# Seven small stores on SyncE's queue for one large store on ScalarE's, in a hybrid transformer block on one core

## The chip, the cores and the metric

The kernel runs on one core of one Trainium2 chip. The metric is the device time of one execution in microseconds. A profiled execution also gives the span, which is the time from its first instruction to its last.

## The reference

One layer with f32 inputs, a sequence of 512 tokens and a model width of 2048. The last three lines are the feed-forward part in which most of the time is spent; there `D_FF` is 5632.

```python
u = rmsnorm(x, attn_norm_w)
z, xbc, dt_raw, q, kc, vc, ks, vs, kw, vw, gate_raw = split(u @ w_in)
y_ssd = ssd_mixer(z, xbc, dt_raw, ...)
y_att = nsa_mixer(q, kc, vc, ks, vs, kw, vw, gate_raw, ...)
h = x + concatenate([y_ssd, y_att]) @ w_out
v = rmsnorm(h, ffn_norm_w)
h = h + (silu(v @ w_gate) * (v @ w_up)) @ w_down
return rmsnorm(h, final_norm_w)
```

## The kernel before

**Arithmetic.** A float32 product is made from three TensorE products of rounded values: each operand is split into a high part (written by ScalarE, line 124) and a low part (the rest, by VectorE, line 127). The three products are the lines 1223 to 1225, or 1219 where they are issued as one stream. The large matrix products are cut into quads of blocks that are multiplied with seven block products instead of eight (Strassen in Winograd's form). So each operand needs seven "forms", sums and differences of its blocks. For a weight, a form is one block as loaded, or a block onto which a second DMA adds another (line 1158 loads on SyncE's queue, line 1160 adds on GpSimd's), or a sum made by GpSimd or VectorE (line 136).

**Stages.** In the trace the input projection and the two mixers take the first 804 us. The output projection (`w_out`) runs from there to 857 us, the gate and up projections to 1735 us, the down projection to about 2180 us, and then the last norm and the output.

**Gate and up.** The 5632 columns are done in `NP` = 22 pairs of 256, about 40 us each. A pair is 14 steps of 16 matmuls. A small scheduler, `Sched`, counts two matmuls as a tick, so that a step has 8 ticks. Jobs such as `g_forms` are generators: `yield n` puts their next part n ticks later. So the ticks fix the order of the instructions on every engine at build time, and on the chip each engine takes its own in that order.

**Forms of a pair.** After a pair, `g_forms(u)` makes the seven forms of its activations, high and low part, in the staging area `ST`, which is part of the tile `A` (slots 44 to 71 of `A`). One DMA of 1792 KB on ScalarE's queue (line 1492) stores all seven to `g_d[u]` in DRAM. The down projection reads them back into a ring with seven slots (`GRING`; slots lie in the tiles `V`, `T` and `u`): pairs 0 to 4 from ScalarE's queue in loads of four and three forms (line 1580), later pairs form by form from SyncE's (line 1598).

**Weights.** `place` gives each coming weight block a buffer in zones of the tiles `Z`, `E` and `A` as soon as one is free, and the load is issued there. `P2["A2"]`, slots 70 to 75 of `A`, is one more zone for the down projection; `down_before` opens it at the visit `v` = 1. The down projection is a written-out list of 35 visits, each with weight blocks 384 to 768 columns wide.

**The output projection's evictions.** `ev_oa(c)`, for c from 0 to 15, adds the residual to a block of `h` (VectorE), stores it to `h_d` (line 1273, 256 KB, on GpSimd's queue), makes the next stage's forms from it, and loads the block c + 4 of the residual into the same buffer (line 1267), which has to wait until the store has read it. Four buffers go round.

**Queues and semaphores.** A DMA queue issues in program order, so what waits at its head holds back all behind it. The DMAs that SyncE and ScalarE issue carry eight completion semaphores in turn, counted over both queues in program order; each is made to wait until the DMA eight before it has landed.

Of the kernel before, what the change touches and what calls it, by code (L numbers as in the profile page):

```python
# [9 lines left out]
F32R = mybir.dt.float32r  # L10
# [7 lines left out]
NP = NFF // 2  # L18
# [7 lines left out]
GRING = 7  # L26
# [88 lines left out]
def body(ctx, tc, xT, w_in, w_out, w_gate, w_up, w_down, w1k, w1v, cols, rows, kst, out):  # L115
    nc = tc.nc
    act, dve, pool, pe = nc.scalar, nc.vector, nc.gpsimd, nc.tensor
    sch = Sched()

    def f(ap):  # L120
        return ap.bitcast(F32)

    def a_hi(dst, src, scale=1.0):
        act.activation(dst, src, AF.Copy, scale=scale)  # L124

    def lo(eng, dst, src, hi):
        eng.tensor_tensor(dst, src, f(hi), ALU.subtract)  # L127

    def neg_lo(dst, src, hi):
        dve.scalar_tensor_tensor(dst, src, -1.0, f(hi), op0=ALU.mult, op1=ALU.subtract)  # L130
# [4 lines left out]
    def add(eng, o, a, b):  # L135
        eng.tensor_tensor(o, a, b, ALU.add)  # L136
# [17 lines left out]
    def ps_v():  # L154
        return ps("v", 1)
# [9 lines left out]
    h_d = dram.tile([NJ, 128, 4, 256], F32, name="h_d")  # L165
    g_d = dram.tile([NP, 7, 128, 512], F32, name="g_d")
# [3 lines left out]
    def open_pool(name, stack=None, **kw):  # L170
        es = ExitStack()
        pools[name] = (es, es.enter_context(tc.tile_pool(name=name, bufs=1, reuse_waits="tile", **kw)))
        return pools[name][1]

    def close_pool(name):
        pools.pop(name)[0].close()
# [95 lines left out]
    def col(c, n=1):  # L272
        return colc[:, c:c + n]
# [311 lines left out]
    P2 = {}  # L585
# [677 lines left out]
    def load_h1(c):  # L1263
        if c < KD:
            P2["h1", c] = (P2["HH"][:, 0:2].rearrange("p a t -> p (a t)"), P2["HH"][:, 2:4].rearrange("p a t -> p (a t)"),
                           P2["SR"].rearrange("p a t -> p (a t)"), rrow)[c % 4]
            (nc.scalar if c < 4 else nc.sync).dma_start(P2["h1", c], h1_d[c])

    def ev_oa(c):
        def ev(p):  # L1270
            h = P2.pop(("h1", c))
            add(dve, h, p, h)
            nc.gpsimd.dma_start(h_d[c // 2][:, 2 * (c % 2):2 * (c % 2) + 2, :].rearrange("p a t -> p (a t)"), h)
            t = P2["t", c % 2] = P2["TT"][:, 2 * (c % 2):2 * (c % 2) + 2].rearrange("p a t -> p (a t)")
            a_hi(t, h, scale=col(C_FN + c))
            if c == 0:
                act.activation(acc2, h, AF.Square)
            else:
                q = ps_v()
                act.activation(q, h, AF.Square)  # L1280
                add(dve, acc2, q, acc2)
            k = c // 2
            if c % 2 == 0:
                a_hi(P2["V0"][:, k, 0, :], t[:, 0:256])
                lo(dve, P2["V0"][:, k, 1, :], t[:, 0:256], P2["V0"][:, k, 0, :])
            else:
                e = P2["t", 0]
                vh, t2 = P2["VV"][:, :, k, 0, :], t.rearrange("p (a t) -> p a t", a=2)
                a_hi(vh, t2)
                lo(dve, P2["VV"][:, :, k, 1, :], t2, vh)  # L1290
                t1, t2 = P2["T1"][k // 4][:, k % 4, :], P2["T2"][:, k, :]
                pool.tensor_tensor(t1, e[:, 256:512], e[:, 0:256], ALU.subtract)
                pool.tensor_tensor(P2["T34"][:, 0, k, :], e[:, 256:512], t[:, 256:512], ALU.subtract)
                pool.tensor_tensor(t2, t1, t[:, 256:512], ALU.subtract)
                pool.tensor_tensor(P2["T34"][:, 1, k, :], t[:, 0:256], t2, ALU.add)
            load_h1(c + 4)
            sch.flags.add(("oa", c))
            if c == 7:
                sch.add(half_t())
        return ev  # L1300
# [14 lines left out]
    def half_t():  # L1315
        yield 12
        t_piece(0, 0)
        yield 16
        t_piece(1, 0)
# [151 lines left out]
    def g_forms(u):  # L1471

        ct = P2["CT"].rearrange("p (s c a) t -> p s c (a t)", s=2, c=2)
        g = ct[:, 1]
        tg = ct[:, 0].rearrange("p a t -> p (a t)").rearrange("p (a t) -> p a t", a=4)
        sg = P2["ST"][:, 0:14, :].bitcast(F32R).rearrange("p (v s) t -> p v s t", s=2)
        yield 10
        a_hi(sg[:, 0, 0, :], g[:, 0, lo_h])
        a_hi(sg[:, 1:3, 0, :], g[:, 1, :].rearrange("p (a t) -> p a t", a=2), scale=-1.0)
        gq = g.rearrange("p c (a t) -> p (c a) t", a=2)  # L1480
        dve.tensor_tensor(tg[:, 1, :], gq[:, 1, :], gq[:, 0, :], ALU.subtract)
        add(dve, tg[:, 2, :], gq[:, 1, :], gq[:, 3, :])
        add(dve, tg[:, 0, :], tg[:, 1, :], gq[:, 3, :])
        dve.tensor_tensor(tg[:, 3, :], tg[:, 0, :], gq[:, 2, :], ALU.subtract)
        yield 4
        lo(dve, sg[:, 0, 1, :], g[:, 0, lo_h], sg[:, 0, 0, :])
        neg_lo(sg[:, 1:3, 1, :], g[:, 1, :].rearrange("p (a t) -> p a t", a=2), sg[:, 1:3, 0, :])
        a_hi(sg[:, 3:7, 0, :], tg)
        yield 4
        lo(dve, sg[:, 3:7, 1, :], tg, sg[:, 3:7, 0, :])  # L1490
        yield 16
        nc.scalar.dma_start(g_d[u].rearrange("v p n -> p v n"), f(sg).rearrange("p v s t -> p v (s t)"))
        sch.flags.add(("g", u))

    PIECES = {1: (1, 1), 4: (2, 0), 5: (2, 1), 7: (3, 0), 9: (3, 1)}
# [75 lines left out]
    def feed(i):  # L1571

        for half, r in ((0, slice(0, 4)), (1, slice(4, 7))):
            while nxt["ring", half] < 5:
                n = nxt["ring", half]
                at = done.get((n - GRING, 0), i) + 1 if half == 0 else done.get((4 - GRING, 0), i) + 3 + n // 2
                if at > i:
                    break
                G[n] = P2["slot"][n]
                nc.scalar.dma_start(f(G[n][:, r]).rearrange("p v s t -> p v (s t)"),  # L1580
                                    g_d[n, r].rearrange("v p n -> p v n"))
                nxt["ring", half] += 1
        if not ring:
            for n in range(5, NP):
                for o in range(7):
                    ring.append((first_use[n, o], n, o, later[n] if n < GRING else freed[n - GRING, o] + 3))
            ring.sort()
        here = [x for x in ring if x[3] <= i]
        tight = any(x[0] - 8 - i < k for k, x in enumerate(here, 1))
        for x in here[:2 if tight else 1]:  # L1590
            ring.remove(x)
            u, n, o, _ = x
            assert u > i + 4
            if n == NP - 1 and not o:
                sch.run_until(("g", n))
            G[n] = P2["slot"][n % GRING]
            a = G_POS[V_OF[SEQ_D[o]]]
            nc.sync.dma_start(f(G[n][:, a]).rearrange("p s t -> p (s t)"), g_d[n, a])
        if not ring:
            ring.append((len(steps) + 99, 0, 0, len(steps) + 99))  # L1600
# [3 lines left out]
    def add_h(v):  # L1604
        j = H_AT.get(v)
        if j is not None:
            assert all(x[0] != j for x in visits[v:v + 2]) and all(any(x[0] == j for x in y) for y in (visits[:v], visits[v + 2:]))
            nc.gpsimd.dma_start(P2["H"][j][:, 1:5, :], h_d[j], accum_op=ALU.add)

    def g_rhs(p, lo_):  # L1610
        a = G_POS[V_OF[p]]
        return lambda k: (G[lo_ + k][:, a, 0, :], G[lo_ + k][:, a, 1, :])
# [155 lines left out]
    def down_before(v, n):  # L1768
        def before():
            if n == 1:  # L1770
                assert v < NJ - 2 or not any(fz.busy[NZ2:])
                add_h(v)
                if v:
                    P2["A2"] = P2["A"][:, 70:76, :]
            elif n == 0 and v == 27:
                x = GRING * 2 + 1
                assert max(i for i, y in enumerate(visits) if y[1] <= x < y[2]) < v
                close_pool("t0")
                P2["X"] = open_pool("t0", side="right").tile([128, 32, 128], F32, name="X")
            elif (v, n) == (0, 0):  # L1780
                close_pool("E")
                P2["E2"] = P2["E"] = open_pool("E").tile([128, NE, 128], F32, name="E2")
        return before
# [13 lines left out]
    for v, (j, a, b) in enumerate(visits):  # L1797
# [14 lines left out]
        for n, p in enumerate(SEQ_D):  # L1812
            blk, sums = q["form"][p]
            if n == 0 and v in (2, 3):
                later[5 + (v == 3)] = len(items)
            s = Step(blk, g_rhs(p, a), bk(p), after=af(p),
                     before=down_before(v, n) if n < 2 else None, sums=sums)
# [54 lines left out]
    with tc.manual_schedule(engines={mybir.EngineType.PE, mybir.EngineType.Activation, mybir.EngineType.DVE}):  # L1872
        for k in range(KD):
            if k % 4 == 0:
                issue_split(k // 4)
            t = xt[:, k, :]
# [113 lines left out]
```

## Time and profile before

| | us |
|---|---|
| median of 3 runs | 2211.69 |
| lowest and highest | 2210.35, 2212.78 |
| the profiled execution | 2210.91 |
| its span | 2209.1 |
| TensorE busy in the span | 2151.5 |
| VectorE busy | 1779.7 |
| ScalarE busy | 1207.5 |
| GpSimd busy | 441.0 |

The mean granted TensorE clock is 0.996 of full speed. TensorE (PE) is busy for 97% of the span; what a change of the DMAs can move is the rest, and what a slow clock behind a gap adds. A line of the waits reads: engine, what it was about to issue, what released it, and then us in total, number of times, the longest. A line of the windows gives for a stretch the busy time of each engine, the granted clock, the mean busy share of the 16 DMA engines (which can come out somewhat over 1) and the rate. A line of the chain is the start, the length and the piece of work that everything after it had to wait for.

### The profile page before, as it was taken

The numbers are of one execution on the slowest core, as the hardware profiler recorded it, in microseconds if no ns is written. First come the engines' busy times: TensorE is split into PE (matmuls) and PEld (weight loads), VectorE is DVE, ScalarE is ACT, GpSimd is POOL, SyncE is SP. The second block draws the span as 40 slices with busy tenths as digits, with TensorE's granted clock in tenths as the row PEclk, the third lists the DMA queues.
The fourth block names the chain that finished last, engine by engine and source line by source line (L and its number), as shares of the span: only waits on it lengthen the run. The fifth ranks groups of instructions, "written<-read, shape, count | busy, mean of one in ns | idle before, by whom it ended". The sixth has DMA issues, their size and how long they took to land.

```text
span 2209.1 us, 35224 instructions
## 1 busy us (share of the span) xinstructions
PE 2151.5 (97%) x12924; PEld 1895.9 (86%) x12924; DVE 1779.7 (81%) x2791; ACT 1207.5 (55%) x2022; POOL 441.0 (20%) x460
## 2 busy tenths in 40 slices
PE   8999999999999999999999999999999999999997
PEld 6888888888788887888888888888888899999997
DVE  6799766878886658888888888888888888887896
ACT  5455456676676657555555555555555444343453
POOL 0002323424431135000000000000000232222232
PEclk9999999999999999999999999999999999999999
DMA  5222342223464467878888888788888879897974
GB/s 201 91 72 70 131 138 88 76 96 108 141 206 115 108 209 208 234 211 254 228 231 239 218 254 228 232 237 215 256 225 225 307 228 305 234 292 207 319 183 114
DMA packets 176141, 427.16 MB, mean 193 GB/s; under 512 B 18608, under 2 KB 25792, under 8 KB 175968
## 3 DMA queue, kind: packets, MB, share of 16 engines
q1 hardware_dynamic: 118592, 283.12, 38.1%
q0 software_dynamic: 30864, 90.09, 20.6%
q10 hardware_dynamic: 26512, 51.70, 6.5%
q8 instruction: 101, 1.65, 0.3%
q14 instruction: 72, 0.59, 0.1%
HBM read 358.78 MB, written 62.39 MB: 191 GB/s over the span
## 4 chain that ended last, share of the span: by engine, by line
PE 80%; DVE 8%; DMA 5%; ACT 4%; issue 3%; POOL 0%; DVEq 0%; SPq 0%; ACTq 0%; POOLq 0%
PE ps_s L1219 19%; PE ps_g L1219 10%; PE ps_g L234 7%; PE ps_g L236 7%; PE ps_g L235 7%; PE ps_t L1219 4%; PE ps_g L1225 2%; PE ps_g L1223 2%; PE ps_g L1224 2%; PE ps_t L1225 2%; PE ps_t L1223 2%; PE ps_t L1224 2%; PE ps_s L1223 2%; PE ps_s L1224 2%; PE ps_s L1225 2%
## 5 line engine op out<-in xcount | busy, mean ns | idle before, releaser
L124 ACT ACTIVATE R<-Z 128x1024 fp32r<-128x1024 f32 (+4 forms) x446 | 407.1, 925 | 418.5 <-DVE Z L136 299.8
L127 DVE TENSOR_TENSOR R<-Z,R 128x1024 fp32r<-128x1024 f32 (+4 forms) x355 | 376.5, 1068 | 28.6 <-ACT R L124 13.3
L234 PE MATMUL ps_g<-u,whi 128*128 128x512 f32 x778 | 320.9, 412 | 0.0
L236 PE MATMUL ps_g<-u,wlo 128*128 128x512 f32 x778 | 305.8, 393 | 0.0
L235 PE MATMUL ps_g<-u,whi 128*128 128x512 f32 x778 | 304.9, 392 | 0.0
L1219 PE MATMUL ps_s<-u,R 128*128 128x512 f32 (+1 forms) x1160 | 252.9, 348 | 8.2 <-ACT A L1428 8.1
L1219 PEld LDWEIGHTS ps_s<-u,R 128*128 128x128 f32 x1160 | 187.7, 188 | 39.7 <-ACT A L1428 13.1
L127 DVE TENSOR_TENSOR wlo<-wraw,whi 128x512 fp32r<-128x512 f32 x211 | 160.5, 762 | 60.9 <-ACT whi L124 59.7
L124 ACT ACTIVATE whi<-wraw 128x512 fp32r<-128x512 f32 x211 | 131.4, 624 | 109.7 <-PE ps_g L235 76.8
L236 PEld LDWEIGHTS ps_g<-u,wlo 128*128 128x128 f32 x778 | 146.1, 188 | 31.8
L234 PEld LDWEIGHTS ps_g<-u,whi 128*128 128x128 f32 x778 | 146.6, 188 | 23.5
L235 PEld LDWEIGHTS ps_g<-u,whi 128*128 128x128 f32 x778 | 147.0, 189 | 21.1
L1219 PE MATMUL ps_t<-u,R 128*128 128x512 f32 (+1 forms) x600 | 131.5, 348 | 0.0
L1219 PE MATMUL ps_g<-u,R 128*128 128x512 f32 x584 | 131.3, 349 | 0.0
L1219 PE MATMUL ps_s<-T,R 128*128 128x512 f32 (+1 forms) x560 | 125.7, 349 | 1.6 <-DVE R L127 1.6
L1219 PE MATMUL ps_g<-T,R 128*128 128x512 f32 (+1 forms) x584 | 126.0, 346 | 0.4 <-DVE R L127 0.4
L1219 PE MATMUL ps_s<-V,R 128*128 128x512 f32 (+1 forms) x568 | 123.8, 348 | 0.6 <-ACT V L124 0.3
L872 ACT ACTIVATE e<-e,em 128x128 f32<-128x128 f32 (+3 forms) x128 | 71.6, 559 | 78.8 <-DVE em L870 78.2
L127 DVE TENSOR_TENSOR E<-Z,R 128x1024 fp32r<-128x1024 f32 (+1 forms) x91 | 111.0, 1219 | 4.5 <-ACT R L124 4.1
L136 DVE TENSOR_TENSOR Z<-Z 128x1024 f32<-128x1024 f32 (+4 forms) x99 | 110.0, 1112 | 4.6 <-POOL Z L136 2.6
L1219 PEld LDWEIGHTS ps_t<-u,R 128*128 128x128 f32 x600 | 98.0, 188 | 14.0
L136 DVE TENSOR_TENSOR A<-ps_g,A 128x512 f32<-128x512 f32 (+1 forms) x102 | 67.3, 664 | 52.2 <-PE ps_g L1219 39.1
(507 smaller groups left out, 5623.5 us busy)
## 6 DMA issues: line engine op xcount, KB each, us to landing
Z<-in_w_up SPq DMA_DIRECT2D x94, 512.0 KB, 5.5
Z<-in_w_gate SPq DMA_DIRECT2D x94, 512.0 KB, 6.7
wraw<-in_w_in SPq DMA_DIRECT2D x164, 256.0 KB, 2.6
g_d<-A ACTq DMA_DIRECT2D x22, 1792.0 KB, 15.1
Z<-in_w_up POOLq DMA_DIRECT2D x37, 512.0 KB, 7.9
Z<-in_w_gate POOLq DMA_DIRECT2D x37, 512.0 KB, 7.2
u<-g_d SPq DMA_DIRECT2D x70, 256.0 KB, 5.5
Z<-in_w_down SPq DMA_DIRECT2D x55, 320.0 KB, 4.7
```

The costliest lines, as they stand in the source:

```text
L124: act.activation(dst, src, AF.Copy, scale=scale)
L127: eng.tensor_tensor(dst, src, f(hi), ALU.subtract)
L136: eng.tensor_tensor(o, a, b, ALU.add)
L234: pe.matmul(p, hi_t[i][:, j, :], ah, start=(k == 0), stop=False)
L235: pe.matmul(p, hi_t[i][:, j, :], al, start=False, stop=False)
L236: pe.matmul(p, lo_t[i][:, j, :], ah, start=False, stop=(k == u.nk - 1))
L872: act.activation(e[:, 0:L], e[:, 0:L], AF.Exp, scale=-1.0, bias=m[:, 0:1], accum_out=m[:, 1:2])
L1219: pe.matmul(o, w, x, start=start, stop=(k == n - 1 and o is q), skip_group_check=not fresh[0])
L1223: pe.matmul(q, h[:, k, :], ah, start=(k == 0), stop=False)
L1224: pe.matmul(q, h[:, k, :], al, start=False, stop=False)
L1225: pe.matmul(q, l[:, k, :], ah, start=False, stop=(k == s.blk.n - 1))
```

## The change

1. `g_forms` stores each form by its own DMA of 256 KB on SyncE's queue, 8 ticks apart, instead of all seven with one DMA of 1792 KB on ScalarE's. The first store comes 8 ticks after the last low part, where the large one came after 16.
2. The second-to-last pair (u = 20) waits another 118 ticks with its stores, which puts them into the down projection.
3. The last pair (u = 21) stages its forms in ring slot 6, in the tile `u`, instead of `ST`, which the pair 20 still holds. The ring's loads into slot 6 (n = 6) therefore wait for that store, and those of pair 20 for its own.
4. The zone `A2` overlaps `ST`, so it is opened at the visit 3 instead of 1. The buffers of the down projection's blocks come out otherwise from there.
5. The stores to `h_d` in `ev_oa` go to ScalarE's queue.

```diff
@@ ev_oa
-            nc.gpsimd.dma_start(h_d[c // 2][:, 2 * (c % 2):2 * (c % 2) + 2, :].rearrange("p a t -> p (a t)"), h)
+            nc.scalar.dma_start(h_d[c // 2][:, 2 * (c % 2):2 * (c % 2) + 2, :].rearrange("p a t -> p (a t)"), h)
@@ g_forms
-        sg = P2["ST"][:, 0:14, :].bitcast(F32R).rearrange("p (v s) t -> p v s t", s=2)
+        if u < NP - 1:
+            sg = P2["ST"][:, 0:14, :].bitcast(F32R).rearrange("p (v s) t -> p v s t", s=2)
+        else:
+            sg = P2["slot"][GRING - 1][:, 0:7]
...
-        yield 16
-        nc.scalar.dma_start(g_d[u].rearrange("v p n -> p v n"), f(sg).rearrange("p v s t -> p v (s t)"))
+        if u == NP - 2:
+            yield 118
+        for v in range(7):
+            yield 8
+            nc.sync.dma_start(g_d[u, v], f(sg[:, v]).rearrange("p s t -> p (s t)"))
@@ feed
-            if n == NP - 1 and not o:
-                sch.run_until(("g", n))
+            if n in (GRING - 1, NP - 2, NP - 1):
+                sch.run_until(("g", n + (n == GRING - 1) * (NP - GRING)))
@@ down_before
-                if v:
+                if v == 3:
+                    sch.run_until(("g", NP - 2))
                     P2["A2"] = P2["A"][:, 70:76, :]
```

On SyncE's queue (SP), in the second and third pair of gate and up. `Z` and `A` are buffers of weight blocks as destinations; `g_d<-A` is a form out of `ST`. Before:

```order
L1158 DMA Z<-in_w_gate 128x1024 x4
L1158 DMA A<-in_w_gate 128x1024
L1158 DMA Z<-in_w_up 128x1024 x5
L1158 DMA Z<-in_w_gate 128x1024
L1158 DMA A<-in_w_gate 128x1024
L1158 DMA Z<-in_w_gate 128x1024 x3
```

and now:

```order
L1158 DMA Z<-in_w_gate 128x1024
L1498 DMA g_d<-A 128x512
L1158 DMA Z<-in_w_gate 128x1024
L1498 DMA g_d<-A 128x512 x2
L1158 DMA Z<-in_w_gate 128x1024
L1498 DMA g_d<-A 128x512 x3
L1158 DMA Z<-in_w_gate 128x1024
L1158 DMA A<-in_w_gate 128x1024
L1498 DMA g_d<-A 128x512
L1158 DMA Z<-in_w_up 128x1024 x5
```

The seven stores of a pair stand among its loads of gate weights, and each load of those waits behind one to three of them on its queue.

On ScalarE (ACT), at the end of the gate and up projections. `V`, `T` and `u` are the ring's slots that the down projection's first forms are loaded into; L1428, L1438 and L1406 are evictions of products. Before, this stood there:

```order
L1580 DMA T_8638<-g_d 128x4x512
L124 ACTIVATE R<-Z 128x1024
L1492 DMA g_d<-A 128x7x512
L1428 ACTIVATE A<-ps_s 128x512
L124 ACTIVATE R<-Z 128x1024
L1428 ACTIVATE A<-ps_g 128x512
L1580 DMA T_8634<-g_d 128x4x512
```

The row L1492, pair 20's store, is gone from ScalarE, and its seven parts now stand on SP at the start of the down projection, in turn with the last pair's (`g_d<-u` out of ring slot 6):

```order
L1158 DMA Z<-in_w_down 128x640 x4
L1498 DMA g_d<-u 128x512
L1498 DMA g_d<-A 128x512
L1498 DMA g_d<-u 128x512
L1498 DMA g_d<-A 128x512
L1498 DMA g_d<-u 128x512
L1498 DMA g_d<-A 128x512
L1498 DMA g_d<-u 128x512
L1498 DMA g_d<-A 128x512
L1604 DMA u<-g_d 128x512
L1158 DMA E_16020<-in_w_down 128x640
```

The ring's loads (L1604, which was L1598) begin behind eight of these stores.

On GpSimd (POOL), late in the output projection; L1292 to L1295 make forms of `h`, L1160 adds weight blocks. Before:

```order
L1160 DMA Z<-in_w_up 128x1024
L1293 TENSOR_TENSOR A<-A 128x256
L1294 TENSOR_TENSOR A<-Z,A 128x256
L1160 DMA Z<-in_w_gate 128x1024
L1273 DMA h_d<-A 128x512
L1295 TENSOR_TENSOR A<-A 128x256
L1292 TENSOR_TENSOR Z<-A 128x256
L1273 DMA h_d<-rrow 128x512
```

and now:

```order
L1160 DMA Z<-in_w_up 128x1024
L1293 TENSOR_TENSOR A<-A 128x256
L1294 TENSOR_TENSOR A<-Z,A 128x256
L1160 DMA Z<-in_w_gate 128x1024
L1295 TENSOR_TENSOR A<-A 128x256
L1292 TENSOR_TENSOR Z<-A 128x256
L1293 TENSOR_TENSOR A<-A 128x256
```

The 16 stores to `h_d` left this engine; on ScalarE each now stands just ahead of the scaled high part of the same block.

## The prediction

> **What bounds the kernel.** I read the first page first, its busy shares and costliest groups, then the waits of TensorE over the whole span, and then, for each wait, the chain, the windows and the DMA issues around it.
>
> ```profile
> span 2209.1 us, 35224 instructions
> PE 2151.5 (97%) x12924; PEld 1895.9 (86%) x12924; DVE 1779.7 (81%) x2791; ACT 1207.5 (55%) x2022; POOL 441.0 (20%) x460
> L1219 PE MATMUL ps_s<-u,R 128*128 128x512 f32 (+1 forms) x1160 | 252.9, 348 | 8.2 <-ACT A L1428 8.1
> g_d<-A ACTq DMA_DIRECT2D x22, 1792.0 KB, 15.1
> ```
>
> TensorE is busy but for 57.6 us (2209.1 − 2151.5), and the change leaves every matmul as it is. So it can win only part of these 57.6 us, and the slow-clock time behind long gaps. The last row is the transfer to be split: 22 stores that take 15.1 us to land. The waits of TensorE that the change can reach are:
>
> ```profile
> PE ps_s L1219 <- ACT A L1428: 8.1, 12, 1.6
> PE ps_t L1225 <- DVE R L127: 5.4, 4, 3.3
> PE ps_g L1223 <- ACT R L124: 3.0, 1, 3.0
> PE ps_g L1223 <- DVE A L136: 2.4, 1, 2.4
> PE ps_g L1225 <- DVE R L127: 2.3, 3, 1.3
> ```
>
> Rows 1 and 2 lie at the gate and up pairs and at their end, rows 3 and 5 for the most part near 2080 us, row 4 in the output projection. Together 21.2 us.
>
> **Part 1, the pairs.** The 12 waits of row 1 stand some 19 us behind a form store's issue. One of them, from ScalarE's timeline (the store's issue), the chain, the timeline again, the chain, the DMA issues (first the accumulating load at 985 us, then that at 996 us), the windows, ScalarE's waits in all pairs and one more of its rows:
>
> ```profile
> 995.02 0.37 ACTq L1492 DMA_DIRECT2D g_d<-A  x1
> 996.61 12.64 DMA Z<-in_w_up
> 1009.34 1.06 ACT L124 ACTIVATE R<-Z 128x1024 fp32r<-128x1024 f32 x1 [2.77 <-DMA Z<-in_w_up]
> 1012.62 1.23 DVE A L136
> Z<-in_w_up POOLq DMA_DIRECT2D x1, 512.0 KB, 7.3
> Z<-in_w_up POOLq DMA_DIRECT2D x1, 512.0 KB, 12.6
> 980.00:995.00 15.00, 15.00 (x89) 13.19 (x88) 13.47 (x17) 8.61 (x12) 0.86 (x1) 1.00 0.70 166
> 995.00:1010.00 15.00, 15.00 (x89) 13.15 (x88) 11.77 (x11) 6.57 (x9) 0.86 (x1) 1.00 0.96 311
> ACT R L124 <- DMA Z<-in_w_up: 34.0, 18, 3.3
> 1205.59 1.07 ACT L124 ACTIVATE R<-A 128x1024 fp32r<-128x1024 f32 x1 [1.14 <-DMA A<-in_w_up]
> 1720.31 2.78 PE ps_g L1219 x16
> ```
>
> A weight block's second, accumulating load on GpSimd's queue takes 12.6 us beside the store, and 7.3 before it. ScalarE waits 2.77 us for it, an eviction on VectorE and ScalarE's L1428 come late behind that, and TensorE stands. At 1205.6 us a ScalarE wait of 1.14 us cost TensorE nothing. So the load may be somewhat late, and only what goes beyond about 1.5 us (an estimate from these two waits and the gaps behind them) is paid.
>
> After the change the 1792 KB leave over 48 ticks from the first store to the last, 17 us at 2.78 us for 16 matmuls (last row) or 8 ticks, instead of at once. In the quiet window (980 to 995 us) the DMA engines are at 0.70 with 166 GB/s; 1.84 MB over 17 us add 108 GB/s, some 0.28 at the 390 GB/s that the full windows below reach. That is 0.98 for as long as the stores run, so the accumulating load will not be back at 7.3; I take 9 to 10 us. This is 3 us less than 12.6, more than the 2.77 by which ScalarE waited. Gain: 7.5 of the 8.1 us, up to 10 with slow first matmuls behind the 12 gaps (an estimate), and 4 if the load only comes down to 11.
>
> The new cost is on SyncE: 154 stores instead of 22 on ScalarE. The nearest rows are the ring's loads of the same size, issued there in 0.384 us (320 to 1973 ns), and SyncE's own waits in the pairs:
>
> ```profile
> L1598 SPq DMA_DIRECT2D u<-g_d x70: 319/384/1973, 1759.7 to 2077.0; - x70
> SPq L1158 <- DVE Z L136: 317.0, 36, 10.5
> ```
>
> 7 × 0.384 = 2.7 us a pair, in a queue that spends 317 us of 800 in one kind of wait alone. The forms are made 8 ticks ahead of the first store, so a store waits for little at the head; it may wait for the DMA eight back, which with 15 DMAs a pair was issued some 20 us earlier. I take 0; the upper end is in the slower rival. ScalarE loses 22 issues of 0.37 us, which ran beside its work: 0.
>
> **Part 2, the end of the gate and up projections.** Pair 20's store is issued at 1707.5 us, among the ring's first loads. Its issue, its landing, that of the last pair's store at 1752.8 us, then windows, chain and one wait of SyncE's:
>
> ```profile
> 1707.46 0.37 ACTq L1492 DMA_DIRECT2D g_d<-A  x1
> g_d<-A ACTq DMA_DIRECT2D x1, 1792.0 KB, 15.6
> g_d<-A ACTq DMA_DIRECT2D x1, 1792.0 KB, 6.5
> 1705.00:1710.00 5.00, 5.00 (x30) 4.13 (x29) 5.00 (x6) 4.73 (x7) 0.21 (x1) 1.00 1.01 300
> 1735.00:1740.00 5.00, 3.27 (x26) 2.87 (x24) 3.66 (x5) 1.01 (x2) 2.63 (x3) 1.00 1.06 382
> 1740.00:1745.00 5.00, 1.87 (x13) 1.87 (x14) 4.87 (x7) 2.56 (x6) 1.66 (x1) 0.93 1.04 388
> 1745.00:1750.00 5.00, 5.00 (x34) 5.00 (x34) 4.97 (x9) 2.78 (x5) 1.05 (x1) 0.73 0.54 184
> 1724.83 12.69 DMA V<-g_d
> 1737.96 0.70 ACT R L124
> SPq L1158 <- DMA g_d<-A: 8.5, 1, 8.5
> ```
>
> The DMA engines are full from 1705 to 1745 us. The chain runs through a ring load of 12.69 us to a ScalarE form that had to wait behind a DMA issue, and TensorE loses 1.7 + 3.1 us, 4.9 by its waits, and runs at 0.73 for 5 us behind that (1.35 us). The last row is a weight load that waited 8.5 us for the store by way of the eight semaphores. The store is 1.84 MB, at 388 GB/s 4.7 us of a full DMA; without it all behind comes up to 4.7 us earlier. But VectorE is busy 4.87 and 4.97 of 5 us right there, so part of the gap would be its. I take 4 of the 6.2 us, between −1 (the same bytes come back at 1747 to 1764 us, beside the last pair's store, in windows with a share of 0.54 and less spare than they seem) and +6. Where they come back, the last pair's store took 6.5 us, so there was room; the ring's loads into slot 6 and of pair 20 wait for them, but stand 30 ticks or more ahead of their first use, over 10 us. I take 0 for that, and at most the 4 us that 1.5 MB too much at 390 GB/s would take.
>
> [...]
>
> **Part 3, the block near 2080 us.** The chain and ScalarE, then two windows:
>
> ```profile
> 2075.05 7.43 DMA Z<-in_w_down
> 2082.57 1.58 ACT L124 ACTIVATE R<-Z 128x768 fp32r<-128x768 f32 x2 [6.66 <-DMA Z<-in_w_down]
> 2080.00:2085.00 5.00, 1.49 (x10) 1.07 (x9) 1.56 (x2) 2.43 (x4) 0.88 (x1) 1.00 1.05 360
> 2085.00:2090.00 5.00, 5.00 (x32) 5.00 (x31) 4.86 (x9) 0.71 (x2) 1.35 (x1) 0.66 1.05 374
> 1984.63 1.59 ACT L124 ACTIVATE R<-Z 128x768 fp32r<-128x768 f32 x2 [1.81 <-DVE Z L136]
> ```
>
> TensorE loses 3.5 us and then a third of 5 us to the clock, 1.7: 5.2 us. The later `A2` changes which buffers come free when: in the program this block's load now stands 46 ticks ahead of its first use, where it stood 26, that is 20 × 0.35 = 7 us earlier, more than ScalarE's 6.66. But another block, whose accumulating load served ScalarE near 1985 to 1987 us just in time, goes from 36 ticks ahead to 26, 3.5 us later, and ScalarE's late forms cost TensorE what goes beyond about 1.5 us: 0 to 3 us, I take 1. Net 4, from +5.2 to −2.
>
> **Part 4, the output projection.** The `h_d` stores leave GpSimd. Its waits, and the chain:
>
> ```profile
> POOL Z L1160 <- DMA Z<-in_w_up: 3.8, 1, 3.8
> 854.13 3.12 DMA A<-h_d
> 857.27 0.70 DVE A L136
> ```
>
> GpSimd stood 3.8 us for a weight load at L1160, with stores behind it that the reload of the same buffer waited for, up to VectorE's add at 857.27 us; TensorE lost 2.4 us (row 4 above). On ScalarE a store goes out as soon as the add that ScalarE waits for anyway is done. The price there is 16 issues beside its work, 0, or a wait for the DMA eight back. I take a gain of 2, from −2 (the same 2.4 once more on ScalarE) to 4.
>
> **Sum.** 7.5 + 4 + 4 + 2 = 17.5 us off 2210.9: 2193.4. The median of the runs was 0.8 above the profiled execution: 2194.2. My own range for this case is 2185 to 2200. ±0.2% of 2211.69, what this measurement tells from no change, is 2207.3 to 2216.1.
>
> **Rivals.**
> *Only the pairs gain.* VectorE, at 4.87 of 5, holds the end of gate and up where it is, and the stall near 2080 moves to 1987. Then 7.5 + 0.5 + 0.5 + 0.5 = 9: 2202.7. For it: VectorE's row at 1740. Against: the wait of 8.5 us for the store itself.
> *No change.* The same bytes go over the same engines (0.98 in my own sum for part 1), and the accumulating loads land as late behind several small stores as behind one large one; gains and losses within 3 us: 2210. For it: the share. Against: 12.6 against 7.3. [...]
> *Slower.* SyncE's order: a store at the head waits for its semaphore or behind a blocked load (10.5 us at the longest), and the gate-weight loads behind one to three stores slip. If two blocks a pair then come as late as 12 of them do now, at 8.1 / 12 = 0.7 us each, 20 pairs lose 27 us; with 10 us won in parts 2 to 4 it is 2228.7. It decides from 0.9 us a pair on (17.5 / 20). For it: the order of the queue. Against: SyncE's long waits are for free buffers, that is, the loads are issued with time to spare.
>
> **Chances.** The forecast 0.52, only the pairs 0.27, no change 0.12, slower 0.09. Faster is the first two and a little of the third, 0.80; same 0.11; slower 0.09. The range goes from 2185, all of 7.5 + 6.2 + 5.2 + 4 and a little, to 2210, with "only the pairs" and half of "no change" in it.
>
> **What would show it.** Part 1: the row of 12 waits for L1428 is gone, and ScalarE's 34.0 us of waits for `Z<-in_w_up` fall to a third; if they stay, the pairs' step is wrong. Part 2: the clock stays at 1.00 in 1745 to 1750 us, and TensorE's wait there is under 2 us. Part 3: no stretch at 0.66 near 2080 us, and no new wait near 1987 us over 1.5 us. Part 4: no wait for VectorE's add at 857 us. A SyncE wait for a `g_d` store that stands ahead of a late weight load would make it wrong on the other side.

## The result and the profile after

The changed kernel takes 2199.45 us (median of 4 runs, 2195.2 to 2199.9), the kernel before 2211.02 beside it: 11.6 us less by the medians. The ratio is 0.9943, with a 95% interval of 0.9927 to 0.9959, which is 12.6 us. On another chip, later, the ratio was 0.9924 (0.9910 to 0.9938). 2194.2 had been predicted, with a range of 2185 to 2210.

From the first page of the changed kernel, and from TensorE's waits over its span:

```profile
span 2193.2 us, 35486 instructions
PE 2146.0 (98%) x12924; PEld 1894.2 (86%) x12924; DVE 1775.3 (81%) x2791; ACT 1210.3 (55%) x2022; POOL 429.7 (20%) x444
L1219 PE MATMUL ps_s<-u,R 128*128 128x512 f32 (+1 forms) x1160 | 251.4, 347 | 0.6 <-ACT A L1428 0.6
g_d<-A SPq DMA_DIRECT2D x147, 256.0 KB, 6.3
PE ps_t L1225 <- DVE R L127: 7.7, 6, 1.9
PE ps_g L1219 <- DVE R L127: 1.9, 1, 1.9
PE ps_t L1223 <- ACT R L124: 1.2, 1, 1.2
PE ps_s L1219 <- ACT A L1428: 0.6, 1, 0.6
```

The 12 waits for L1428 are down to one of 0.6 us. That one was the first of the 12 (at 915.0 us before, 911.4 now). It comes ahead of the first form store in both kernels (915.7 and 913.6 us), so a store can't have caused it. The waits of `ps_t` for VectorE's `R` went up from 5.4 to 7.7 us: 3.8 at the end of gate and up, 2.0 near 1760 us and 1.9 between 2083 and 2093 us. In the pairs, ScalarE's wait for accumulating loads (34.0 us before), and the one such load that now runs beside the third pair's stores, at 991.5 us (before: 12.6 us, at 996.6):

```profile
ACT R L124 <- DMA Z<-in_w_up: 4.5, 5, 2.1
Z<-in_w_up POOLq DMA_DIRECT2D x1, 512.0 KB, 9.8
```

The busy shares don't say where 15.7 us went. TensorE issues the same 12924 matmuls in both kernels (one of them some places later), so the time at which the same matmul in order starts can be compared, and the differences of these times over a stretch of the program say what that stretch won or lost. For the profiled runs against that of the kernel before, in us, by stretches of the kernel before:

| kernel | 800–950 | 950–1700 | 1700–1755 | 1755–1800 | 1800–2075 | 2075–2110 |
|---|---|---|---|---|---|---|
| changed | −3.0 | −10.7 | 0.0 | +2.2 | +0.2 | −3.0 |
| e_after_again (the same) | −3.9 | −10.7 | −0.3 | +2.1 | +1.0 | −1.0 |
| e_hd | +0.4 | +3.0 | +1.1 | −0.6 | +0.6 | +0.8 |
| e_pairs | −1.5 | −10.6 | +0.2 | +0.8 | +1.1 | +0.3 |
| e_hd_pairs | −1.4 | −10.7 | +1.2 | −0.4 | +0.7 | −0.1 |
| e_last_act | 0.0 | −10.7 | +0.9 | +2.1 | +1.4 | −0.9 |
| e_pairs_act | −1.6 | −10.8 | +0.5 | +0.3 | +0.6 | 0.0 |
| e_big_sp | −0.8 | −10.6 | +2.0 | +0.3 | +1.5 | +0.3 |
| e_burst_sp | 0.0 | −10.7 | +1.6 | −0.6 | +1.3 | −0.2 |
| e_burst_act | +0.6 | −9.8 | +1.0 | −1.0 | +1.3 | −0.3 |
| e_a2 | −1.8 | −10.5 | +0.1 | +0.5 | +0.5 | −1.8 |
| e_a2_again | −0.7 | −10.7 | +0.1 | +0.6 | +1.8 | −2.8 |
| e_ring_lite | −1.7 | −10.7 | −2.1 | +2.9 | +0.9 | +0.3 |

Of the changed kernel's four runs the profiled one is the shortest, 2195.2 at a granted clock of 0.996; the others took 2199.3 to 2199.9 at 0.993 to 0.994. So its trace shows 15.7 us where the medians show 11.6.

The column 950–1700 has +3.0 for e_hd, which stores its pairs as the kernel before does. What the late loads cost thus differs by 3 us between two traces of the same arrangement. The 12 traces whose pairs are stored in another way lie within 1 us of each other there.

### The profile page after: what moved, and what is told of

It reads as the page before. It is cut to its first block, busy times and chain, and to the rows that moved or that the text cites. A ratio compares the mean times of both kernels' runs of the same rounds, so it can differ in the third digit from the quotient of the medians.

```text
span 2193.2 us, 35486 instructions
## 1 busy us (share of the span) xinstructions
PE 2146.0 (98%) x12924; PEld 1894.2 (86%) x12924; DVE 1775.3 (81%) x2791; ACT 1210.3 (55%) x2022; POOL 429.7 (20%) x444
## 5 line engine op out<-in xcount | busy, mean ns | idle before, releaser
L127 DVE TENSOR_TENSOR R<-Z,R 128x1024 fp32r<-128x1024 f32 (+4 forms) x359 | 384.8, 1080 | 32.5 <-PE ps_t L1219 7.8
L127 DVE TENSOR_TENSOR wlo<-wraw,whi 128x512 fp32r<-128x512 f32 x211 | 160.1, 760 | 60.9 <-ACT whi L124 59.8
L127 DVE TENSOR_TENSOR E<-Z,R 128x1024 fp32r<-128x1024 f32 (+1 forms) x91 | 111.5, 1225 | 7.1 <-PE ps_t L1219 3.4
L136 DVE TENSOR_TENSOR Z<-Z 128x1024 f32<-128x1024 f32 (+4 forms) x96 | 104.5, 1088 | 6.7 <-POOL Z L136 5.3
L1219 PEld LDWEIGHTS ps_g<-T,R 128*128 128x128 f32 x584 | 94.9, 188 | 15.6 <-DVE R L127 2.3
```

Source lines behind the costliest of these rows:

```text
L1219: pe.matmul(o, w, x, start=start, stop=(k == n - 1 and o is q), skip_group_check=not fresh[0])
```

## The experiments

**The four parts.** First, one part of the change each, on one chip (5 rounds; the kernel before took 2213.3 there).

*e_hd: only the `h_d` stores on ScalarE's queue.*

```diff
-            nc.gpsimd.dma_start(h_d[c // 2]...
+            nc.scalar.dma_start(h_d[c // 2]...
```

> The kernel before with one edit: the stores to h_d on ScalarE's queue. If the 4.1 us that the changed kernel gains between 800 and 900 us come from GpSimd no longer holding these stores behind its wait for a weight load, this kernel gains the same 4 us in that stretch (about 2207), and TensorE's waits of 2.4 us for VectorE's add and of 1.6 us for VectorE's R are gone. Rival: the 4.1 us come from elsewhere in the change or from chance; then the stretch stays within 1 us.

Measured: 2211.3, ratio 0.9992 (0.9980 to 1.0005). The waits between 800 and 950 us, in this kernel:

```profile
PE ps_g L1223 <- DVE A L136: 1.3, 2, 1.1
PE ps_g L1219 <- DVE R L127: 1.3, 1, 1.3
PE ps_m L282 <- DVE acc L136: 0.9, 1, 0.9
PE ps_g L1223 <- ACT ps_v L1280: 0.9, 1, 0.9
```

The wait of 1.6 us is gone and that of 2.4 us halved. But one of 1.3 us came at 903 us, in the second pair, and one of 0.9 us at L1280 (the one for `acc` was there before, with 0.8), and the stretch is 0.4 us longer. The 4.1 us that I had read off one pair of traces between 800 and 900 us are not the effect of this edit alone. In the table the column 800–950 runs from −3.9 to +0.4 with the edit and from −1.8 to +0.6 without it. What these stores are worth was not settled.

*e_pairs: only the split stores, on SyncE's queue, for pairs 0 to 19.*

```diff
+        if u < NP - 2:
+            for v in range(7):
+                yield 8
+                nc.sync.dma_start(g_d[u, v], f(sg[:, v])...)
+        else:
             yield 16
             nc.scalar.dma_start(g_d[u]...)
```

> The kernel before with one edit: pairs 0 to 19 store each form by its own DMA of 256 KB on SyncE's queue, 8 ticks apart; pairs 20 and 21 keep their one store on ScalarE's queue, from the staging area. If the 9.7 us gained between 900 and 1700 us are these stores alone, this kernel gains 9 to 10 us (about 2201.5) and the 12 waits of 8.1 us for L1428 fall under 1 us. Rival, that the moved last pairs or the h_d stores carry part of it: under 6 us.

Measured: 2198.65, ratio 0.9940 (0.9926 to 0.9954). That is the changed kernel's whole gain, with one of its four parts. The column 950–1700 shows −10.6 (13.6 less than in e_hd), and no wait for L1428 is left after 912 us.

*e_hd_pairs: both of these, without the part on the last two pairs.*

> The changed kernel without its last-pair part (pairs 20 and 21 as in the kernel before, A2 opened at visit 1). The prediction put the moved last pairs at 4 us for the end of gate and up and 4 us near 2080; then this kernel is about 8 us slower than the changed one, 2203 to 2207. The comparison of the two traces says that they are worth nothing net (0 at the end of gate and up, +3 near 1760, -2 near 2080); then it is at 2195 to 2199, with TensorE's waits of 4.9 us at the end of gate and up, and the one of 3.0 us near 2080, back.

Measured: 2198.44, ratio 0.9939 (0.9924 to 0.9954), on a par with the changed kernel. TensorE's waits at the end of gate and up, and near 2080 us, are the old ones:

```profile
PE ps_t L1225 <- DVE R L127: 5.0, 2, 3.5
PE ps_g L1223 <- ACT R L124: 2.9, 1, 2.9
```

So moving the last pairs' stores and opening `A2` later takes the wait near 2080 us away, spreads the one of 5.0 us (3.8 and, a little later, 0.9 in the changed kernel), and pays as much elsewhere.

**Where it is paid.** In the changed kernel the DMA engines stand nearly still from 1745 to 1750 us and are full 10 us later, when TensorE waits; GpSimd's sum of two blocks waits for a load, VectorE for the sum. Windows, then GpSimd and VectorE:

```profile
1745.00:1750.00 5.00, 5.00 (x45) 5.00 (x44) 4.76 (x8) 3.05 (x7) 0.00 (x0) 1.00 0.13 46
1760.00:1765.00 5.00, 3.01 (x23) 2.60 (x22) 4.07 (x7) 1.62 (x3) 0.93 (x2) 1.00 1.05 407
1759.20 1.57 POOL L136 TENSOR_TENSOR Z<-Z 128x640 f32<-128x640 f32 x1 [2.59 <-DMA Z<-in_w_down]
1760.80 0.82 DVE L136 TENSOR_TENSOR Z<-Z 128x640 f32<-128x640 f32 x1 [3.51 <-POOL Z L136]
```

*e_last_act: the last two pairs' 14 stores on ScalarE's queue.*

```diff
-            nc.sync.dma_start(g_d[u, v], ...)
+            (nc.sync if u < NP - 2 else nc.scalar).dma_start(g_d[u, v], ...)
```

> The changed kernel with the 14 stores of pairs 20 and 21 on ScalarE's queue instead of SyncE's, all else alike. In the changed kernel the DMA engines are at 0.13 from 1745 to 1750 us and full from 1750 to 1765, and TensorE then loses 3 us. If the stores and ring loads were held back behind a weight load that waits for its buffer at the head of SyncE's queue, the stores now run in that quiet stretch, and the waits near 1760 us fall from 2.6 us to under 1: 2 to 3 us faster than the changed kernel. Rival: the bytes of that stretch don't fit whatever the queue; then the waits stay at 2 to 3 us. Second rival: ScalarE is held by the stores' semaphores and forms come late: new waits of TensorE for ScalarE between 1735 and 1770.

Measured: 2197.32, ratio 0.9937 (0.9921 to 0.9953), as the changed kernel. The loss stayed: +2.1 in the column 1755–1800. The waits and a window:

```profile
PE ps_t L1225 <- DVE R L127: 1.5, 2, 1.1
1765.00:1770.00 5.00, 3.48 (x27) 3.07 (x27) 4.43 (x7) 1.98 (x5) 0.92 (x2) 1.00 1.05 399
```

This run decides less than it was meant to. In the changed kernel eight of the 14 stores were already issued ahead of the quiet stretch (1737.4 to 1741.8 us), and six from 1749.5 us on. Here nine were issued by 1753.6 us, and five (1754.4 to 1758.4) still fell into the full stretch. So the edit hardly changed how many stores fall there. It shows that changing the queue doesn't help; it doesn't tell stores that are held back from too many bytes at once. e_a2, below, takes the stores away.

**Why the split helps.** Three properties changed at once for a pair's store: one DMA or seven, which queue, at once or over 17 us. Four kernels have them apart, each against the kernel before (3 rounds).

*e_pairs_act: seven stores over 17 us, still on ScalarE's queue (`nc.scalar` in e_pairs).*

> As e_pairs, but the seven small stores of pairs 0 to 19 stay on ScalarE's queue: the split and its spread in time without the change of queue. If what counts is that the 1792 KB no longer come at once, this gains as much as e_pairs (about 13 us, ratio 0.994) and the waits for L1428 are under 1 us. If what counts is that the stores share SyncE's queue with the loads instead of taking a third queue's share, at most half of it is gained and several of the 12 waits stay. ScalarE's risk: an issue that waits for the DMA eight back holds its forms; then new waits of TensorE for ScalarE.

*e_big_sp: one store, on SyncE's queue.*

```diff
-        nc.scalar.dma_start(g_d[u].rearrange(...
+        (nc.sync if u < NP - 2 else nc.scalar).dma_start(g_d[u].rearrange(...
```

> The kernel before with one edit: the one store of 1792 KB of pairs 0 to 19 on SyncE's queue. The change of queue without the split. If the split is what counts: the accumulating load stays at over 12 us, or SyncE's loads now wait behind 1792 KB on their queue and are late by up to 5 us, so no gain, 2208 to 2220. If the queue is what counts: the gain of e_pairs, about 2200.

*e_burst_sp: seven stores back to back where the one stood, on SyncE's queue (`yield 16` ahead of the first, none between).*

> As e_pairs, but the seven stores are issued back to back, 16 ticks after the last low part, where the large store stood: split and queue without the spread in time. If the spread is what counts: the waits for L1428 are back at 4 us or more, and the time at 2205 or more. If many small packets or the queue are what counts: as e_pairs, waits under 1 us, ratio 0.994.

*e_burst_act: the same seven back to back on ScalarE's queue.*

> As e_burst_sp, but the seven stores go back to back on ScalarE's queue: split alone, with the third queue and the burst kept. If a burst on a queue of its own beside SyncE's and GpSimd's is what slows the accumulating loads, over 10 of those in the pairs take more than 11 us again and TensorE's waits for L1428 come back at 4 us or more (2205 to 2212). If the size of the single DMA is what counts, this gains as e_pairs does: no more than one load over 11 us, waits under 1 us, ratio 0.994.

| kernel | us | ratio (95%) | accumulating loads over 11 us, of 80 or 81 |
|---|---|---|---|
| before | 2212.2, 2215.5 | | 17 |
| e_pairs_act | 2200.99 | 0.9944 (0.9929–0.9959) | 0 |
| e_big_sp | 2203.45 | 0.9954 (0.9939–0.9969) | 0 |
| e_burst_sp | 2200.99 | 0.9948 (0.9931–0.9965) | 0 |
| e_burst_act | 2201.21 | 0.9934 (0.9908–0.9960) | 2 |

The last column is counted from the DMA records between 915 and 1700 us. No single one of the three properties is needed: each of the four kernels gains. The stretch 950–1700 is 9.8 to 10.8 us shorter in all of them. The stores themselves didn't become fast; they land late still where they come in a burst or large. From e_burst_act and e_big_sp:

```profile
g_d<-A ACTq DMA_DIRECT2D x140, 256.0 KB, 10.0
g_d<-A SPq DMA_DIRECT2D x20, 1792.0 KB, 12.8
```

What they share is that the accumulating load beside a pair's stores takes 1.5 to 2.4 us less: its median is 11.5 us before, 10.0 in e_burst_act, 9.6 in e_pairs and in the changed kernel, 9.5 in e_pairs_act, 9.2 in e_big_sp and e_burst_sp. Only what ScalarE waits beyond some 1.5 us reaches TensorE. Side by side in the trace before, ScalarE's waits of 3.14, 2.77, 2.05 and 1.88 us are followed by waits of TensorE of 1.59, 1.23, 0.51 and 0.35 us, each 1.53 to 1.55 less. The waits were 1.9 us in the mean (34.0 / 18) and 3.3 at most. So a small relief takes away the whole stall, whichever way it comes.

A fourth property changed without being asked for: the order of issue. Before, the store goes out 1.6 us ahead of the accumulating load; in e_big_sp and e_burst_sp it stands behind two weight loads on SyncE's queue and goes out 1.0 us after it. Timelines, before and e_big_sp:

```profile
995.02 0.37 ACTq L1492 DMA_DIRECT2D g_d<-A  x1
996.61 0.86 POOL L1160 DMA_DIRECT2D Z<-in_w_up  x1 [9.88 <-DMA Z<-in_w_up]
994.78 0.86 POOL L1160 DMA_DIRECT2D Z<-in_w_up  x1 [14.28 <-DMA Z<-in_w_up]
995.76 0.43 SPq L1492 DMA_DIRECT2D g_d<-A  x1
```

By the median pair, 1792 KB of stores are issued ahead of the accumulating load in the kernel before, 1024 in e_burst_act, 512 in e_pairs_act, 256 in e_pairs and the changed kernel, and none in e_big_sp and e_burst_sp. The load's time falls in nearly the same order, from 11.5 to 9.2 us. So the bytes that go out just ahead of the load fit all the runs; no run changes them alone, and this reading isn't shown.

**Which half of the last-pair part does what.** *e_a2: e_pairs, with `A2` opened at visit 3 and the last pairs stored as before.*

```diff
-                if v:
+                if v == 3:
                     P2["A2"] = P2["A"][:, 70:76, :]
```

> As e_pairs, but the zone A2 opens at visit 3 as in the changed kernel, with pairs 20 and 21 stored as before. If the later A2 alone moves the buffers so that weight loads wait at the head of SyncE's queue near 1750 us: the changed kernel's loss of 3 us between 1755 and 1800 is here, and its shift near 2080 (-5.6 between 2075 and 2090, then +2.6) too. If the 14 stores in that stretch cause the loss: none of it here.

Measured: 2198.28, ratio 0.9934 (0.9915 to 0.9952). The column 1755–1800 has +0.5 and 2075–2110 has −1.8. So the change near 2080 us is that of `A2` alone. All six traces with the later `A2` win 5.6 us between 2075 and 2090 us and lose 2.6 to 5.9 in the 20 us behind it. The loss near 1760 needs the moved last pairs: their 14 stores, the staging in ring slot 6 and the ring loads that wait for them, which no run takes apart. In e_a2 the last store, of 1792 KB, goes out at 1740.1 us, ahead of the quiet stretch. The same window as above, in this kernel:

```profile
1745.00:1750.00 5.00, 5.00 (x45) 5.00 (x44) 4.88 (x9) 2.38 (x5) 0.00 (x0) 1.00 0.19 69
1760.00:1765.00 5.00, 5.00 (x45) 5.00 (x43) 4.87 (x7) 3.21 (x7) 1.57 (x1) 1.00 0.82 300
```

The quiet stretch is here too, at 0.19. (In the changed kernel a weight load on SyncE's queue waits 5.8 us for VectorE's `R`, L127, and goes out at 1749.1 us, the next store after it at 1749.5.) Without the stores what follows runs at 0.82 instead of 1.05, and TensorE is not held up. In the table +2.1 to +2.9 stands in that column for all four kernels with the moved stores, and at most +0.8 for the others.

**Why the end of gate and up didn't gain.** *e_ring_lite: the changed kernel with the ring's ten loads at the end of gate and up cut to a quarter.*

```diff
-  nc.scalar.dma_start(f(G[n][:, r])..., g_d[n, r]...)
+  nc.scalar.dma_start(f(G[n][:, r])...[:, :, 0:128], g_d[n, r]...[:, :, 0:128])
```

> The changed kernel, but the ring's ten loads on ScalarE's queue at the end of gate and up bring only a quarter of each form's columns (6.6 MB less; the rest of the slots keeps old values). If the end of gate and up is bound by DMA bandwidth, which the move of pair 20's store relieved by too little, TensorE's waits between 1715 and 1737 us fall from 4.7 us to under 1.5 and the clock stays at 1.00 there. If VectorE and GpSimd are the bound (VectorE's multiplications there took 2.0 to 2.3 us beside GpSimd's sums, instead of 1.2), or the weight loads that wait for buffers, the waits stay at 3.5 us or more.

Measured: 2198.58, ratio 0.9920 (0.9898 to 0.9942). In the changed kernel, windows and VectorE:

```profile
1715.00:1720.00 5.00, 5.00 (x33) 4.49 (x32) 3.81 (x4) 0.46 (x2) 1.57 (x1) 1.00 0.99 365
1720.00:1725.00 5.00, 3.12 (x21) 2.91 (x20) 3.29 (x3) 2.09 (x4) 3.49 (x3) 0.85 0.89 287
1725.00:1730.00 5.00, 3.05 (x20) 2.76 (x19) 4.84 (x8) 2.01 (x5) 1.08 (x1) 0.81 0.91 327
1717.57 2.32 DVE L133 TENSOR_TENSOR A<-A,rrow 128x1024 f32<-128x1024 f32 x1
1721.71 0.82 DVE L136 TENSOR_TENSOR Z<-Z 128x640 f32<-128x640 f32 x1 [1.82 <-POOL Z L136]
```

With a quarter of the ring's bytes, windows and TensorE's waits from 1710 to 1740 us (in the changed kernel 3.8 and 0.9):

```profile
1720.00:1725.00 5.00, 3.73 (x30) 3.32 (x28) 4.97 (x6) 1.88 (x4) 2.25 (x2) 1.00 0.74 223
1725.00:1730.00 5.00, 3.40 (x17) 3.40 (x18) 4.83 (x11) 4.10 (x8) 0.00 (x0) 0.70 0.44 131
PE ps_t L1225 <- DVE R L127: 2.9, 2, 2.5
```

The DMA engines now have room, the weight loads at 1714 to 1715 us land in 2.9 to 3.6 us instead of 6.3 to 8.0, and VectorE is busy 4.97 and 4.83 of 5 us. Waits of 2.9 us and a clock of 0.70 remain. The result is between the two expectations: 1.8 us of the waits (4.7 to 2.9) were DMA. The larger part stays while VectorE is nearly full; that VectorE is its cause is likely, but no run makes VectorE's work less. If three quarters of ten ring loads win 1.8 us, pair 20's store of 1.84 MB could not win 4.

**The two candidates side by side.** The stages pointed to e_a2 as better than the changed kernel, so both ran on one chip (5 rounds).

> The changed kernel once more, for a direct comparison with e_a2_again on one chip: ratio to the kernel before near 0.994, 2.6 us lost between 1700 and 1800 us against the kernel before and 5.6 won near 2080. It was taken before in runs of 2195.2 at a granted clock of 0.996 and of 2199.5 at 0.993 to 0.994; if the profile falls on 0.993 or 0.994, the windows show where the clock was low.

> e_a2 once more beside the changed kernel: split stores for pairs 0 to 19 and the late A2, without the moved stores of the last two pairs and with the h_d stores on GpSimd's queue. By the stages of the traces it has the 10 us of the pairs and the 2 us near 2080, without the 3 us lost near 1760: 2 to 3 us faster than the changed kernel, if the h_d stores are worth nothing. Rival: the h_d stores win some 2 us between 800 and 900, as the prediction put it; then the two kernels are alike within 1 us.

Measured: the changed kernel 2197.41, ratio 0.9924 (0.9910 to 0.9938); e_a2 2200.06, ratio 0.9940 (0.9926 to 0.9954). The 2 to 3 us did not come; e_a2 has no lead. In the traces what e_a2 saves near 1760 (1.4 us) it loses between 800 and 950 us (3.3). That fits the rival on the `h_d` stores, but the same column differs by as much between runs of one kernel or nearly one (e_a2 twice: −1.8 and −0.7; with the stores on ScalarE −3.9 to +0.4), so it isn't shown. No kernel here is clearly faster than the changed one.

The second trace of the changed kernel also shows a part of its spread. Near 2090 us, windows and the wait; first the profile at 2195.2 us, then the later one at 2197.6:

```profile
2090.00:2095.00 5.00, 3.40 (x27) 2.99 (x26) 2.79 (x5) 4.87 (x9) 2.32 (x2) 1.00 0.60 133
2095.00:2100.00 5.00, 5.00 (x44) 5.00 (x44) 4.90 (x8) 0.92 (x2) 2.16 (x2) 1.00 0.59 121
```

```profile
PE ps_t L1223 <- ACT R L124: 2.3, 1, 2.3
2090.00:2095.00 5.00, 2.39 (x18) 1.98 (x17) 1.75 (x3) 4.78 (x8) 1.75 (x2) 1.00 0.62 133
2095.00:2100.00 5.00, 5.00 (x31) 5.00 (x31) 3.63 (x7) 1.68 (x3) 2.16 (x2) 0.66 0.63 79
```

The wait is 2.3 us where it was 1.2, and behind it the clock is 0.66 for 5 us, which costs another 1.7 us. What makes up the rest of the 2 to 4 us between runs was not looked into.

## Why the prediction was right, and where it was not

The time lies in the range, 5.3 us above the forecast. By mechanism, though, it is the rival "only the pairs gain" (2202.7), with a larger gain there, and that rival is nearer, by 2 us. The range held both, so that the time lies in it says nothing for parts 2 to 4. In part it is luck: the pairs were taken 3 us too low, parts 2 and 3 with the stores' cost near 1760 us 7 to 9 us too high.

**Part 1, the pairs: right, undersized.** 7.5 us were taken, up to 10 with the slow first matmuls; 10.7 were won. I had put the accumulating load at 9 to 10 us, and it came at 9.6. The term that was mis-sized is the cost of a gap. Ten of the 12 waits, 7.2 us, lie in the stretch 950–1700; by the starts of the matmuls TensorE loses 0.17 us more at each of them and 0.11 a step later, 9.9 us in all, and the other 0.8 in gaps of under 0.3 us. The first of the 12 waits was no store's, as shown above, so "some 19 us behind a form store's issue" is not true of that one. ScalarE's waits fell from 34.0 to 4.5 us, further than to the third that was to show it. The price of 0 for SyncE's queue held: no wait of TensorE in the pairs goes back to a `g_d` store, and the slower rival did not come.

How long the stores themselves took is not what counted. The seven of 256 KB landed in 6.3 us each where one of 1792 KB took 15.1; but nobody waits for either in the pairs, and e_big_sp, with the large store, gained nearly as much. It was another transfer's landing that counted. The accumulating load beside the stores took 11.5 us by the median with the large store on ScalarE's queue, and 9.2 with the same store on SyncE's (e_big_sp). But the order of issue changed there as well; and e_burst_act, on ScalarE's queue and with 10.0 us, shows that the queue is not all.

**Part 2, the end of gate and up: wrong by 4 us, and by 2 more.** The step that failed is "without it all behind comes up to 4.7 us earlier". The DMA engines got a little room in that part of the program (1.06 and 1.04 before, 0.89 and 0.91 now). But TensorE still waits 3.8 us there and 0.9 us a little later, instead of 4.9, and the clock, which was to stay at 1.00, falls to 0.85 and 0.81: 0.0 and −0.3 us instead of −4. By e_ring_lite even 6.9 MB less (427.2 to 420.3 in all) win no more than some 2 us. The first rival had named VectorE's 4.87 of 5; now it is busy 4.84 us in the second of these windows, and in the first it waits 1.8 us for GpSimd's sum. Which of these holds the rest stays open. And the stores that came back at the start of the down projection, which I priced at 0 with at most 4, cost 2.1 to 2.2 us near 1760.

**Part 3, near 2080: right in kind, too high.** The block named is on time and 5.6 us are won where its stall was. The other block that I had feared for near 1987 costs nothing. But 2.6 to 4.6 us are lost behind it, where forms of other blocks now come late: in the changed kernel TensorE waits 1.5 us for VectorE's `R` at 2083.0 us and 1.2 us for ScalarE's at 2092.2. Net 1.0 to 3.0 instead of 4, and 0.9 us less if what is lost between 2000 and 2075 us is counted too. I had followed two blocks through the shifted buffers and should have followed all of those up to 2110 us.

**Part 4, the output projection: not shown.** 2 us were taken; e_hd says 1.8 us less, with an interval from 4.4 less to 1.1 more, and its trace shows waits given back at the next stage's start.

In sum 17.5 were predicted, of which 7.5 from the pairs. The runs give 11.6 by the medians and 12.6 by the ratio, and e_pairs shows that the pairs alone give that.

## What to carry to other kernels

A large store that nobody waits for can still cost time, through the loads that it delays: look at what else lands late while it is in flight, and how much of that lateness is slack. If only the last 2 us of a load's lateness reach TensorE, any small relief takes the whole stall, so the cheapest edit does; and relief where another engine is already busy for 4.9 of 5 us was worth little here. Read stage by stage before crediting a part of a change: a difference of 4 us in one pair of traces between 800 and 900 us was within what the stretch does anyway.

## What the runs showed that was not expected

VectorE's multiplication of 128 × 1024 took 2.32 us at 1717.6 us, while GpSimd summed two blocks (first row, in the changed kernel); before, the same took 1.23 us where GpSimd stood still (second row):

```profile
1717.24 1.57 POOL L136 TENSOR_TENSOR Z<-Z 128x640 f32<-128x640 f32 x1 [26.49 <-DMA Z<-in_w_down]
1732.36 1.23 DVE L133 TENSOR_TENSOR A<-A,rrow 128x1024 f32<-128x1024 f32 x1
```

Which of VectorE's operations is held up depends on when the sum begins: before, it began at 1728.9 us, ahead of an earlier operation, and that one, a sum of 128 × 512, took 1.62 us instead of 0.69. The trace of the changed kernel also shows which of the two waits. Thirteen of VectorE's subtractions of 128 × 640 (line 127) began while an operation of GpSimd on two tensors had over 0.2 us to go: all of them ended 0.68 to 0.69 us after that operation did, and took up to 2.20 us. Eleven began before GpSimd's operation and took 0.81 to 0.83 us, as they do alone; GpSimd's ten sums of 128 × 640 that began during a subtraction of line 127 took 1.61 to 2.06 us, against 1.56 to 1.58 for the others. So in this trace, with these operations, the engine that begins second is held up.

In these traces the clock's answer to a gap can't be told from its length: near 2090 us it was 1.00 behind a wait of 1.2 us and, in e_a2, behind one of 2.1, but 0.66 over 5 us behind 2.3; and in the changed kernel it fell to 0.85 and 0.81 with two waits of 1.9 us, 5.4 us apart.
